# Late modulation vectors of a diffusion layer: from a matmul with ones to accumulating transfers and a row in DRAM

## The chip, the cores and the metric

The kernel runs on one core of a Trainium2 chip. The metric is the device time of one execution in microseconds, the median of several runs of the program. A profiled execution of the same program gives the trace; its time is given beside its span, which is the stretch from its first to its last instruction.

The engines are named as the profile names them: PE (TensorE matmul), PEld (its weight load), DVE (VectorE), ACT (ScalarE), POOL (GpSimd) and SP (SyncE, which only issues transfers here). POOL issues a few transfers as well.

## The reference

One layer with two token mixers and an MLP, on 256 latent tokens and 256 context tokens of 2048 channels. What concerns the change is how a conditioning vector becomes six modulation vectors of 2048 values each, and where four of them are used:

```python
mod = (jax.nn.silu(c) @ w_mod[l] + b_mod[l])[:, None, :]
sa, ca, ga, sm, cm, gm = jnp.split(mod, 6, axis=-1)
...
h = modulate(x, norm_attn_w[l], sa, ca)
p = h @ w_in[l]
...
x = x + ga * mix
x = x + gm * sq_relu_mlp(modulate(x, norm_mlp_w[l], sm, cm), w_ff1[l], w_ff2[l])
```

`modulate(x, w, shift, scale)` is `rmsnorm(x, w) * (1 + scale) + shift`. So `ga` and `gm` scale the two branches, `sm` shifts the MLP's input, and `cm` enters as `norm_mlp_w * (1 + cm)`. All inputs are float32.

## The kernel before

Tokens or weight columns are held in tiles of 128 partitions; almost all PE time goes into weight products. A weight chunk of 128 x 1024 float32 is loaded by SP into one of five `raw` buffers (`raw_chunk`), then split into a high part `whi` (an ACT cast to the matmul's float format, L243) and a low part `wlo` (a DVE subtraction, L244), each in three buffers. A product then takes three matmuls: high by high, low by high and high by low. The order of the chunks is the list `stream`; `wchunk` hands out the next one, loads two ahead, and calls `tick`, which counts down a list of delayed pieces of work (`later(n, fn)` puts one there, to be emitted n chunks later).

The instructions of one engine run in the order of the program on that engine. A scheduler chooses that order when the program is built, from the order of emission and its own estimate of times; `pin` keeps an instruction of an engine where it was emitted. Engines wait for each other through semaphores, and an instruction that waits holds everything behind it on its engine.

The stages in order of time are: the early modulation `sa`, `ca` together with the first q and k products (to about 122 us), values, keys, queries and attention, the pooling branch (`pin`, `za`, `pd`), the gates and up projections (`pg`, `pyy`), the output projection (`wo`), and the MLP (`f`, with first layer `ff1` and second layer `ff2` alternating in eight blocks).

The other four vectors are made late, in the shade of those stages, by `late_gen`. It works through `ga`, `cm`, `sm`, `gm`, each in two halves of 1024 columns. For a half it:

- clears an accumulator `macc` of 128 x 1024 on POOL (L618) and loads the bias into its partition 0 by a POOL transfer (L619);
- loads 16 weight chunks between those of `stream`, and adds each, times the 128 values of silu(c) that belong to it (one per partition, `sil`), into `macc` on DVE (`late_part`, L637). Afterwards the vector is the sum of `macc` over its partitions;
- splits `macc`, 512 columns at a time, into a high part `ah` (ACT, L270) and a low part `al` (DVE, L271), and multiplies both by a matrix of ones on PE into a PSUM bank (`late_sum`, L656 and L657). That sums over partitions and leaves the sum in all 128 at once;
- copies the bank to its place (ACT, L661), or, for `cm`, adds 1 and multiplies by the norm weight (DVE, L659). The norm weight `nmw` comes as four loads of 128 x 512, already repeated over partitions.

There is one `macc`, so a half can begin only when the half before it has been split. The results stand in `ga_bc`, `sb` (`cm` and `sm`) and `gm_bc`.

POOL does little: the last addition of the rotary embedding on q and k (`qraw`, L485), the clamp of squared attention outputs (`osq`, L740), the running sums of the pooling branch (`za`, L797 to L804), and the squares of the MLP (`rsq`, L1058). After such a square ACT casts it into the next block's operand `act` (L270), between its weight casts.

Of the kernel before, what the change touches and what calls it, by code (L numbers as in the profile page):

```python
# [48 lines left out]
def layer(ctx: ExitStack, tc, a, out):  # L49
    nc = tc.nc  # L50
    pool = ctx.enter_context(tc.tile_pool(name="sb", bufs=1))
    psum = ctx.enter_context(tc.tile_pool(name="ps", bufs=8, space=bass.MemoryType.PSUM))
    pe, gp = nc.tensor, nc.gpsimd
# [17 lines left out]
    def bank(name):  # L71
        return psum.tile([P, 512], F32, tag="ps", name=name)

    def work(name, shape=None, dt=F32):
        return pool.tile(shape or [P, 512], dt, tag="w2", name=name, bufs=9)
# [20 lines left out]
    def later(n, fn):  # L96

        waiting.append([n, fn])
# [170 lines left out]
    def split(hi, lo, src):  # L269
        act.copy(hi, src)  # L270
        vec.tensor_sub(lo, src, hi.bitcast(F32))  # L271
# [36 lines left out]
    ones = pool.tile([P, P], F32R, tag="ones", name="ones")  # L308
    vec.memset(ones.bitcast(F32), 1.0)
# [286 lines left out]
    parts = []  # L596

    def late_gen():
        for name in ("ga", "cm", "sm", "gm"):
# [11 lines left out]
            for half in range(2):  # L611
                yield
                for part in parts:
                    if part in waiting:
                        waiting.remove(part)
                        part[1]()
                acc = pool.tile([P, 1024], F32, tag="macc", name="macc", bufs=1)
                gp.memset(acc, 0.0)  # L618
                nc.gpsimd.dma_start(acc[0:1, :], a["b_" + name][half])  # L619
                norm_w = []  # L620
                for k in range(KT):
                    raw = raw_chunk(a["w_" + name][half, k])
                    if name == "cm" and k == 8:
                        for q in range(2):
                            norm_w.append(work("nmw"))
                            nc.gpsimd.dma_start(norm_w[q], a["nmw"][2 * half + q])
                    later(2 if credit_rate[0] < 1 else 1, partial(late_part, acc, raw, k))
                    parts.append(waiting[-1])
                    if k == KT - 1:
                        o = dst[:, half * 1024:half * 1024 + 1024]  # L630
                        later(2 if credit_rate[0] < 1 else 1, partial(late_split, acc, norm_w, o))
                        parts.append(waiting[-1])
                    yield

    def late_part(acc, raw, k):

        pin(vec.scalar_tensor_tensor(acc, raw, sil[:, 0, k:k + 1], acc, ALU.mult, ALU.add))  # L637

    def late_split(acc, norm_w, o):
        for q in range(2):  # L640
            part = partial(late_half, q, acc, norm_w, o)
            if q == 0:
                part()
            else:
                later(2, part)
                parts.append(waiting[-1])

    def late_half(q, acc, norm_w, o):
        ah, al = work("ah", dt=F32R), work("al", dt=F32R)
        split(ah, al, acc[:, q * 512:q * 512 + 512])  # L650
        later(3, partial(late_sum, ah, al, norm_w[q] if norm_w else None, o[:, q * 512:q * 512 + 512]))

    def late_sum(ah, al, wr, o):

        ps = bank("late")
        pin(pe.matmul(ps, ones, ah, start=True, stop=False))  # L656
        pe.matmul(ps, ones, al, start=False, stop=True)  # L657
        if wr is not None:
            vec.scalar_tensor_tensor(o, ps, 1.0, wr, ALU.add, ALU.mult)  # L659
        else:  # L660
            act.copy(o, ps)  # L661
# [452 lines left out]
def _layout(inp):  # L1114
# [17 lines left out]
    put("nmw", np.broadcast_to(f["norm_mlp_w"][0].reshape(4, 1, 512), (4, P, 512)))  # L1132
# [65 lines left out]
```

## Time and profile before

| What | Value |
|---|---|
| Time, median of 3 runs | 1466.71 us (1464.83 to 1470.06) |
| The profiled execution's own time | 1468.97 us |
| Its span | 1467.0 us |
| PE busy | 1442.9 us |
| DVE busy | 998.5 us |
| ACT busy | 684.7 us |
| POOL busy | 120.9 us |
| Moved by SP's queue | 345.51 MB |
| Moved by POOL's queue | 1.08 MB |

A group line of the profile reads: line, engine, operation, output <- inputs, shape, count, then busy time, mean length of one in ns, and the engine's idle time just before, with what ended it. A line of the timeline begins with the start and the length in us. Matmuls overlap in the pipeline, so the distance between their starts, not their length, is what one costs.

### The profile page before, as it was taken

What the parts mean: (1) busy time and instruction counts of PE and PEld (TensorE: products, weight loads), DVE (VectorE), ACT (ScalarE), POOL (GpSimd) and SP (SyncE); (2) the same over time, 40 slices, a digit from 0 to 9 for tenths busy, and PEclk for the clock granted to TensorE, in tenths of its full rate; (3) what the DMA queues carried; (4) which work ended last, traced back from release to release, by engine and by line L of the source; (5) the groups of instructions that cost most, each with busy time, mean ns of one, the idle gap of its engine ahead of it and who ended that gap; (6) DMA issues with size and microseconds to landing.
All of it is one profiled execution on the core that took longest, in us unless ns stands there. A gap on an engine that the chain in (4) does not pass through costs nothing.

```text
span 1467.0 us, 19801 instructions
## 1 busy us (share of the span) xinstructions
PE 1442.9 (98%) x7480; PEld 1186.6 (81%) x7480; DVE 998.5 (68%) x1239; ACT 684.7 (47%) x929; POOL 120.9 (8%) x120
## 2 busy tenths in 40 slices
PE   6999999999999999999999999999999999999998
PEld 4667887778878888888888888888888888888887
DVE  4568787768887786778676656666666655555675
ACT  5225346466554444445444554445344453544442
POOL 0001110101400000000001000001000000000260
PEclk9999999999999999999999999999999999999999
DMA  9996774435788878899646777777777655556554
GB/s 380 408 408 224 227 277 155 150 110 172 235 288 289 304 267 294 280 318 321 203 168 204 230 246 234 237 225 234 240 241 237 201 189 193 191 190 195 183 196 140
DMA packets 97439, 347.85 MB, mean 237 GB/s; under 512 B 11072, under 2 KB 11712, under 8 KB 97344
## 3 DMA queue, kind: packets, MB, share of 16 engines
q1 hardware_dynamic: 96768, 345.51, 69.8%
q8 instruction: 58, 0.95, 0.3%
q0 software_dynamic: 576, 1.08, 0.2%
q14 instruction: 37, 0.30, 0.1%
HBM read 344.45 MB, written 2.10 MB: 236 GB/s over the span
## 4 chain that ended last, share of the span: by engine, by line
PE 84%; DMA 9%; DVE 5%; ACT 1%; issue 1%; SPq 0%; POOL 0%; DVEq 0%; ACTq 0%; POOLq 0%
PE f L1047 14%; PE f L454 8%; PE f L455 8%; PE f L460 8%; PE f L1050 7%; DMA raw<-in_w_m_dram 6%; PE pg L454 3%; PE pg L455 3%; PE pg L460 3%; PE wo L454 2%; PE pyy L454 2%; PE wo L460 2%; PE pyy L460 2%; PE wo L455 2%; PE pyy L455 2%; PE v L455 2%
## 5 line engine op out<-in xcount | busy, mean ns | idle before, releaser
L244 DVE TENSOR_TENSOR wlo<-raw,whi 128x1024 fp32r<-128x1024 f32 (+1 forms) x430 | 534.7, 1245 | 345.3 <-ACT whi L243 321.8
L243 ACT CAST whi<-raw 128x1024 fp32r<-128x1024 f32 (+1 forms) x430 | 449.8, 1047 | 555.1 <-PE f L455 179.6
L1047 PE MATMUL f<-h,whi 128*128 128x512 f32 x896 | 224.3, 392 | 0.0
L455 PE MATMUL f<-whi,act 128*128 128x512 f32 x512 | 199.3, 389 | 0.0
L454 PE MATMUL f<-whi,act 128*128 128x512 f32 x512 | 199.3, 389 | 0.0
L1047 PEld LDWEIGHTS f<-h,whi 128*128 128x128 f32 x896 | 161.6, 189 | 29.2
L637 DVE SCALAR_TENSOR_TENSOR macc<-raw,sil,macc 128x1024 f32<-128x1024 f32 x128 | 164.9, 1289 | 3.1 <-issue 2.4
L460 PE MATMUL f<-wlo,act 128*128 128x512 f32 x512 | 136.8, 389 | 0.0
L1050 PEld LDWEIGHTS f<-h,wlo 128*128 128x128 f32 x896 | 122.2, 190 | 8.7
L1050 PE MATMUL f<-h,wlo 128*128 128x256 f32 x896 | 124.9, 282 | 0.0
L460 PEld LDWEIGHTS f<-wlo,act 128*128 128x128 f32 x512 | 96.1, 188 | 20.0
L455 PEld LDWEIGHTS f<-whi,act 128*128 128x128 f32 x512 | 96.2, 188 | 19.8
L454 PEld LDWEIGHTS f<-whi,act 128*128 128x128 f32 x512 | 96.2, 188 | 19.8
L454 PE MATMUL pg<-whi,hL 128*128 128x512 f32 x256 | 101.5, 396 | 0.0
L455 PE MATMUL pg<-whi,hL 128*128 128x512 f32 x256 | 100.3, 392 | 0.0
L1058 POOL TENSOR_TENSOR rsq<-relu 128x512 f32<-128x512 f32 x28 | 29.2, 1042 | 527.5 <-ACT relu L1057 497.0
L460 PE MATMUL pg<-wlo,hL 128*128 128x512 f32 x256 | 68.6, 390 | 0.0
L454 PEld LDWEIGHTS pg<-whi,hL 128*128 128x128 f32 x256 | 48.6, 190 | 10.5 <-ACT whi L243 0.2
L455 PEld LDWEIGHTS pg<-whi,hL 128*128 128x128 f32 x256 | 48.5, 189 | 10.4 <-issue 0.2
L460 PEld LDWEIGHTS pg<-wlo,hL 128*128 128x128 f32 x256 | 48.0, 188 | 10.4 <-DVE wlo L244 0.4
L618 POOL MEMSET macc<- 128x1024 f32 x8 | 7.6, 955 | 488.6 <-DVE al L271 375.4
L1072 DVE TENSOR_TENSOR acc<-f,acc 128x512 f32<-128x512 f32 x48 | 30.9, 686 | 19.6 <-PE f L460 19.6
(275 smaller groups left out, 2104.9 us busy)
## 6 DMA issues: line engine op xcount, KB each, us to landing
raw<-in_w_ff_dram SPq DMA_DIRECT2D x240, 512.0 KB, 4.1
raw<-in_w_m_dram SPq DMA_DIRECT2D x64, 512.0 KB, 10.2
raw<-in_w_ga_dram SPq DMA_DIRECT2D x32, 512.0 KB, 4.5
raw<-in_w_cm_dram SPq DMA_DIRECT2D x32, 512.0 KB, 4.6
raw<-in_w_gb_in_dram SPq DMA_DIRECT2D x32, 512.0 KB, 4.7
raw<-in_w_ga_in_dram SPq DMA_DIRECT2D x32, 512.0 KB, 5.1
raw<-in_w_sm_dram SPq DMA_DIRECT2D x32, 512.0 KB, 4.9
raw<-in_w_o_dram SPq DMA_DIRECT2D x32, 512.0 KB, 4.4
```

The source lines that it names most:

```text
L243: act.copy(hi, raw)
L244: vec.tensor_sub(lo, raw, hi.bitcast(F32))
L454: pe.matmul(banks[t], tok(h, k, 0, tt), wt, start=k == 0, stop=False)
L455: pe.matmul(banks[t], tok(h, k, 1, tt), wt, start=False, stop=False)
L460: pe.matmul(banks[t], tok(h, k, 0, tt), wt, start=False, stop=k == 2 * nk - 1)
L618: gp.memset(acc, 0.0)
L637: pin(vec.scalar_tensor_tensor(acc, raw, sil[:, 0, k:k + 1], acc, ALU.mult, ALU.add))
L1047: pe.matmul(ps, hi[:, kk * P:kk * P + P], both(h2, k), start=k == 0, stop=False)
L1050: pe.matmul(ps[:, T:2 * T], lo[:, kk * P:kk * P + P], act_slice(h2, k, 0), start=False, stop=k == KT - 1)
L1058: gp.tensor_mul(sq, r, r)
L1072: vec.tensor_add(acc[:, t, gs], bs[t], acc[:, t, gs])
```

## The change

The products of `late_part` now go straight into the half of `ga_bc`, `sb` or `gm_bc` where the result belongs; `macc` and its splitting, the matrix of ones and the matmuls are gone. The sum over partitions is made by seven transfers that POOL issues: the upper 64 partitions are added onto the lower 64, then 32 onto 32, and so on to one (`late_fold`). For `cm`, POOL adds 1 to that one row and multiplies it by the norm weight, which is now loaded as a row. The row is then written to DRAM (`row`) and read back into all 128 partitions. Each of these steps is emitted one chunk after the last, and each waits for the one before to have landed.

```diff
+    rows = ctx.enter_context(tc.tile_pool(name="rows", bufs=2, space=bass.MemoryType.DRAM))
...
-    ones = pool.tile([P, P], F32R, tag="ones", name="ones")
-    vec.memset(ones.bitcast(F32), 1.0)
...
-                for part in parts:
-                    if part in waiting:
-                        waiting.remove(part)
-                        part[1]()
-                acc = pool.tile([P, 1024], F32, tag="macc", name="macc", bufs=1)
-                gp.memset(acc, 0.0)
-                nc.gpsimd.dma_start(acc[0:1, :], a["b_" + name][half])
-                norm_w = []
+                o = dst[:, half * 1024:half * 1024 + 1024]
+                gp.memset(o, 0.0)
+                nc.gpsimd.dma_start(o[0:1, :], a["b_" + name][half])
+                norm_w = None
                 for k in range(KT):
                     raw = raw_chunk(a["w_" + name][half, k])
                     if name == "cm" and k == 8:
-                        for q in range(2):
-                            norm_w.append(work("nmw"))
-                            nc.gpsimd.dma_start(norm_w[q], a["nmw"][2 * half + q])
-                    later(2 if credit_rate[0] < 1 else 1, partial(late_part, acc, raw, k))
+                        norm_w = pool.tile([P, 1024], F32, tag="macc", name="nmw", bufs=1)[0:1, :]
+                        nc.gpsimd.dma_start(norm_w, a["nmw"][half])
+                    later(2 if credit_rate[0] < 1 else 1, partial(late_part, o, raw, k))
                     if k == KT - 1:
-                        later(2 if credit_rate[0] < 1 else 1, partial(late_split, acc, norm_w, o))
+                        later(2 if credit_rate[0] < 1 else 1, partial(late_fold, o, norm_w, P // 2))
...
-    def late_sum(ah, al, wr, o):
-        ps = bank("late")
-        pin(pe.matmul(ps, ones, ah, start=True, stop=False))
-        pe.matmul(ps, ones, al, start=False, stop=True)
-        if wr is not None:
-            vec.scalar_tensor_tensor(o, ps, 1.0, wr, ALU.add, ALU.mult)
-        else:
-            act.copy(o, ps)
+    def late_fold(o, norm_w, n):
+        if n > 0:
+            nc.gpsimd.dma_start(o[0:n, :], o[n:2 * n, :], accum_op=ALU.add)
+            later(1, partial(late_fold, o, norm_w, n // 2))
+            return
+        if norm_w is not None:
+            gp.tensor_scalar(o[0:1, :], o[0:1, :], 1.0, None, ALU.add)
+            gp.tensor_mul(o[0:1, :], o[0:1, :], norm_w)
+        row = rows.tile([1, 1024], F32, tag="row", name="row")
+        nc.gpsimd.dma_start(row, o[0:1, :])
+        later(1, lambda: nc.gpsimd.dma_start(o, row.broadcast_to([P, 1024])))
```

The new code lies 21 lines higher in most of the program, so L1058 is L1037 there, and L740 is L719. On PE the order of everything else is the same as before. This is PE in the gate stage, where the first half of `cm` is summed; `pg0` and `pg1` are the two banks of a gate product. Before:

```order
L460 MATMUL pg0_3991<-wlo_4037,hL1_731 128x512
L460 MATMUL pg1_3992<-wlo_4037,hL1_731 128x512
L656 MATMUL late_4108<-ah_4041,ones_70 128x512
L657 MATMUL late_4108<-al_4042,ones_70 128x512
L454 MATMUL pg0_3991<-whi_4059,hL1_731 128x512
L455 MATMUL pg0_3991<-whi_4059,hL1_731 128x512
L454 MATMUL pg1_3992<-whi_4059,hL1_731 128x512
L455 MATMUL pg1_3992<-whi_4059,hL1_731 128x512
```

The same place in the changed program:

```order
L459 MATMUL pg0_3974<-wlo_4020,hL1_731 128x512
L459 MATMUL pg1_3975<-wlo_4020,hL1_731 128x512
L453 MATMUL pg0_3974<-whi_4039,hL1_731 128x512
L454 MATMUL pg0_3974<-whi_4039,hL1_731 128x512
L453 MATMUL pg1_3975<-whi_4039,hL1_731 128x512
L454 MATMUL pg1_3975<-whi_4039,hL1_731 128x512
```

The pair of `late` between two weight chunks is gone, and the next chunk follows directly.

POOL's queue around the end of `ga`'s second half, where the pooling branch begins (`za` are its running sums, `osq` the clamped squares of attention outputs). Before:

```order
L740 TENSOR_SCALAR osq_2577<-osq_2577 128x512
L618 MEMSET macc_2926 128x1024
L619 DMA macc_2926<-in_b_cm_dram 1x16x64
L797 MEMSET za_2990 128x8
L798 MEMSET za_2990 128x8
L797 MEMSET za_2995 128x8
L798 MEMSET za_2995 128x8
L740 TENSOR_SCALAR osq_2917<-osq_2917 128x512
L804 TENSOR_TENSOR za_2990<-za_2990 128x271
```

In the changed program, where the folds of 64 and 32 partitions stand just ahead of the first row:

```order
L632 DMA ga_bc_1338<-ga_bc_1338 16x1024
L632 DMA ga_bc_1338<-ga_bc_1338 8x1024
L632 DMA ga_bc_1338<-ga_bc_1338 4x1024
L612 MEMSET sb_2805 128x1024 x2
L613 DMA sb_2805<-in_b_cm_dram 1x16x64
L776 MEMSET za_2974 128x8
L777 MEMSET za_2974 128x8
L776 MEMSET za_2979 128x8
L777 MEMSET za_2979 128x8
L632 DMA ga_bc_1338<-ga_bc_1338 2x1024
L719 TENSOR_SCALAR osq_2904<-osq_2904 128x512
L613 DMA sb_2805<-in_b_cm_dram 1x16x64
```

Five folds now stand ahead of the clearing of `sb` and of the bias load of `cm`, and a sixth ahead of the second `osq`.

POOL's queue in the MLP, around the end of `gm`'s second half. Before, only the squares stand there:

```order
L1058 TENSOR_TENSOR rsq2_9503<-relu_9504 128x512
L1058 TENSOR_TENSOR rsq2_9609<-relu_9610 128x512
L1058 TENSOR_TENSOR rsq2_10042<-relu_10043 128x512
L1058 TENSOR_TENSOR rsq2_10145<-relu_10146 128x512
L1058 TENSOR_TENSOR rsq2_10248<-relu_10249 128x512
```

In the changed program:

```order
L1037 TENSOR_TENSOR rsq2_9559<-relu_9560 128x512
L632 DMA gm_bc_6629<-gm_bc_6629 64x1024
L632 DMA gm_bc_6629<-gm_bc_6629 32x1024
L632 DMA gm_bc_6629<-gm_bc_6629 16x1024
L632 DMA gm_bc_6629<-gm_bc_6629 8x1024
L632 DMA gm_bc_6629<-gm_bc_6629 4x1024
L632 DMA gm_bc_6629<-gm_bc_6629 2x1024
L632 DMA gm_bc_6629<-gm_bc_6629 1x16x64
L639 DMA row_9916<-gm_bc_6629 16x1x64
L1037 TENSOR_TENSOR rsq2_9986<-relu_9987 128x512
L640 DMA gm_bc_6629<-row_9916 128x1024
L1037 TENSOR_TENSOR rsq2_10089<-relu_10090 128x512
```

Seven folds and the write of the row come between two squares, the second of which ACT waits for; the read back comes between the next two.

More of the change, by code (lines that the diff above doesn't have):

```diff
@@ L595, in layer @@
     ga_bc = s8("ga_bc", [P, D])
-    parts = []
     def late_gen():
@@ L623, in late_gen @@
                     if name == "cm" and k == 8:
-                        for q in range(2):
-                            norm_w.append(work("nmw"))
-                            nc.gpsimd.dma_start(norm_w[q], a["nmw"][2 * half + q])
-                    later(2 if credit_rate[0] < 1 else 1, partial(late_part, acc, raw, k))
-                    parts.append(waiting[-1])
+                        norm_w = pool.tile([P, 1024], F32, tag="macc", name="nmw", bufs=1)[0:1, :]
+                        nc.gpsimd.dma_start(norm_w, a["nmw"][half])
@@ L629, in late_gen @@
+                    later(2 if credit_rate[0] < 1 else 1, partial(late_part, o, raw, k))
                     if k == KT - 1:
-                        o = dst[:, half * 1024:half * 1024 + 1024]
-                        later(2 if credit_rate[0] < 1 else 1, partial(late_split, acc, norm_w, o))
-                        parts.append(waiting[-1])
+                        later(2 if credit_rate[0] < 1 else 1, partial(late_fold, o, norm_w, P // 2))
                     yield
-    def late_part(acc, raw, k):
-        pin(vec.scalar_tensor_tensor(acc, raw, sil[:, 0, k:k + 1], acc, ALU.mult, ALU.add))
@@ L639, in late_split @@
[L639 to L643, printed above, removed]
-            else:
[L645 to L651, printed above, removed]
@@ L653, in late_sum, with late_part @@
-    def late_sum(ah, al, wr, o):
-        ps = bank("late")
-        pin(pe.matmul(ps, ones, ah, start=True, stop=False))
-        pe.matmul(ps, ones, al, start=False, stop=True)
-        if wr is not None:
-            vec.scalar_tensor_tensor(o, ps, 1.0, wr, ALU.add, ALU.mult)
-        else:
-            act.copy(o, ps)
+    def late_part(o, raw, k):
+        pin(vec.scalar_tensor_tensor(o, raw, sil[:, 0, k:k + 1], o, ALU.mult, ALU.add))
+    def late_fold(o, norm_w, n):
[9 more added lines that the diff above has]
+        later(1, lambda: nc.gpsimd.dma_start(o, row.broadcast_to([P, 1024])))
@@ L1131, in _layout @@
         put("b_" + n, bm[chunk[n]].reshape(2, 1, 1024))
-    put("nmw", np.broadcast_to(f["norm_mlp_w"][0].reshape(4, 1, 512), (4, P, 512)))
+    put("nmw", f["norm_mlp_w"][0].reshape(2, 1, 1024))
     wi = f["w_in"][0]
```

## The prediction

> **What bounds the kernel now.** I read the page first: busy time by engine and the chain that ended last.
>
> ```profile
> span 1467.0 us, 19801 instructions
> PE 1442.9 (98%) x7480; PEld 1186.6 (81%) x7480; DVE 998.5 (68%) x1239; ACT 684.7 (47%) x929; POOL 120.9 (8%) x120
> PE 84%; DMA 9%; DVE 5%; ACT 1%; issue 1%; SPq 0%; POOL 0%; DVEq 0%; ACTq 0%; POOLq 0%
> ```
>
> TensorE is busy 98% of the span and holds 84% of the chain; POOL holds 0% of it. A stage view shows where that is complete.
>
> ```profile
> 398.00:440.00 42.00, 39.04 (x170) 31.40 (x170) 34.79 (x40) 22.15 (x27) 1.19 (x2) 0.97 0.86 291
> 440.00:760.00 320.00, 319.99 (x1426) 263.88 (x1425) 236.67 (x244) 145.57 (x173) 5.72 (x9) 1.00 0.81 274
> 760.00:1160.00 400.00, 400.00 (x2024) 339.95 (x2024) 262.13 (x272) 191.94 (x237) 23.73 (x22) 1.00 0.71 230
> ```
>
> The columns are the length, then PE, PEld, DVE, ACT and POOL busy, the granted clock, the DMA share and GB/s. From 440 to 1160 us PE has no idle time: a matmul that goes away there is time that goes away, provided nothing new makes PE wait. At 398 to 440 us PE is idle for 3 us and the transfers are at their densest, 0.86.
>
> **What goes: 32 matmuls.** Next I looked at the tile `late`, its times in windows, and PE's timeline around one pair.
>
> ```profile
> L656 PE MATMUL late<-ah,ones 128*128 128x512 f32 x16 | 6.8, 426 | 2.1 <-ACT ah L270 2.1
> 440.00:760.00 320.00, 4.66 (x14) 2.55 (x14) 2.24 (x4) 2.36 (x4) 1.00 0.81 274
> 760.00:1160.00 400.00, 2.54 (x8) 1.50 (x8) 0.00 (x0) 2.35 (x4) 1.00 0.71 230
> 206.30 0.62 PE L460 MATMUL k<-wlo,hC 128*128 128x512 f32 x2
> 206.75 0.40 PE L656 MATMUL late<-ah,ones 128*128 128x512 f32 x1
> 206.99 0.40 PE L657 MATMUL late<-al,ones 128*128 128x512 f32 x1
> 207.22 0.39 PE L454 MATMUL k<-whi,hL 128*128 128x512 f32 x1
> 207.45 0.39 PE L455 MATMUL k<-whi,hL 128*128 128x512 f32 x1
> ```
>
> The mean of 426 ns is the pipelined length, not the price. The price is the distance of starts: from 206.75 to 207.22 a pair takes 0.47 us. The two windows (here of the tile alone) hold 14 + 8 = 22 of the 32 matmuls, so 11 pairs lie where PE never idles: 11 x 0.47 = **5.2 us**, the firmest term. Of the five others, four belong to the gate vector `ga` (200 to 330 us) and one, the first pair of `cm`, stands at 436 us:
>
> ```profile
> 433.67 1.05 ACT L243 CAST whi<-raw 128x1024 fp32r<-128x1024 f32 x1 [2.29 <-DMA raw<-in_w_ga_in_dram]
> 434.95 1.04 ACT L243 CAST whi<-raw 128x1024 fp32r<-128x1024 f32 x1 [0.23 <-DMA raw<-in_w_ga_in_dram]
> 435.90 1.14 ACT L270 CAST ah<-macc 128x512 fp32r<-128x512 f32 x2
> 433.38 1.07 PE L460 MATMUL pg<-wlo,hL 128*128 128x512 f32 x4
> 436.57 0.50 PE L656 MATMUL late<-ah,ones 128*128 128x512 f32 x1 [2.12 <-ACT ah L270]
> 437.91 0.80 PE L657 MATMUL late<-al,ones 128*128 128x512 f32 x1 [0.84 <-DVE al L271]
> 438.50 0.63 PE L454 MATMUL pg<-whi,hL 128*128 128x512 f32 x1
> 438.93 0.63 PE L455 MATMUL pg<-whi,hL 128*128 128x512 f32 x1
> 441.02 0.39 PE L454 MATMUL pg<-whi,hL 128*128 128x512 f32 x1
> ```
>
> Four matmuls from 433.38 at 0.227 us would let the next one start at 434.29; it starts at 438.50, 4.2 us later, because PE, in order, stands at `late` until ACT and DVE have made its two operands. Behind it six matmuls start 0.42 us apart until 441.02 (2.52 us for what takes 1.36): another 1.2 us after the idle time. Together 5.4 us. Without the pair PE next waits for the cast that ends at 433.67 + 1.05 = 434.72, so at most 4.9 us come back. The lower bound is the plain 0.47 us, if the transfers of that stage then hold PE anyway. The following cast (434.95) was ready before PE, a chunk of 12 matmuls or 2.7 us later, would ask for it, so I take **4.5 us**, near the upper end. The four `ga` pairs are worth 4 x 0.47 = 1.9 us at most, but all come before the cast at 433.67 that waited for a weight transfer, so the gain may only lengthen that wait: 0 to 1.9, I take **0.3**. The casts `ah`, the differences `al` and the copies out of PSUM leave ACT and DVE, which are idle 53% and 32% of the time; I count nothing for that (at best one DVE weight difference less in front of a chunk, about 1.2 us, at worst as much lost by a changed order). Sum of the gains: 5.2 + 4.5 + 0.3 = **10.0 us**.
>
> **What comes: 72 transfers on POOL's queue, each waiting for the last.** A half now takes seven accumulating folds, one write of the row and one broadcast, in POOL's program order with POOL's other work. No accumulating transfer is in the trace; the nearest rows are POOL's own small loads:
>
> ```profile
> L619 POOL DMA_DIRECT2D macc<-in_b_gm_dram x2: 487/514/540, 683.0 to 955.4; - x2
> DMA to landing us min/median/max: 1.8/3.7/5.2
> nmw<-in_nmw_dram POOLq DMA_DIRECT2D x4, 256.0 KB, 4.7
> ```
>
> An issue costs POOL about 0.5 us; a 4 KB load lands 1.8 to 5.2 us after its issue, a 256 KB load after 4.7. A fold moves 256, 128, ... 4 KB. So a step, issue to next issue, is bounded by 1.9 and 5.3 us; I take **3.8** (the median and a tenth for the semaphore), since most folds are as small as those loads. POOL elsewhere has long gaps (8% busy); two places decide. First the second half of `gm`:
>
> ```profile
> 1138.38 1.28 DVE L637 SCALAR_TENSOR_TENSOR macc<-raw,sil,macc 128x1024 f32<-128x1024 f32 x1
> 1167.90 1.04 POOL L1058 TENSOR_TENSOR rsq<-relu 128x512 f32<-128x512 f32 x1 [54.53 <-ACT relu L1057]
> 1168.98 0.62 ACT L270 CAST act<-rsq 128x512 fp32r<-128x512 f32 x1 [0.21 <-POOL rsq L1058]
> 1170.15 1.05 ACT L243 CAST whi<-raw 128x1024 fp32r<-128x1024 f32 x1 [0.55 <-PE f L1047]
> 1168.06 2.00 PE L1047 MATMUL f<-h,whi 128*128 128x512 f32 x8
> 1170.86 2.00 PE L1047 MATMUL f<-h,whi 128*128 128x512 f32 x8
> 1176.44 2.00 PE L1047 MATMUL f<-h,whi 128*128 128x512 f32 x8
> ```
>
> The last product lands in the sum at 1139.66. Seven folds and the issue of the row stand ahead of the square of 1167.90 in POOL's order; two `late` pairs fall away in between, so the square is due at 1166.96. That is 27.3 us, 3.9 us a step for no delay. If the square is late, ACT stands at its cast of it, and the weight cast of 1170.15 queues behind. PE takes a chunk every 2.80 us and `whi` has three buffers, so that cast is for the chunk of 1176.44 and has 1176.44 - 1171.20 = 5.2 us to spare. PE loses from (27.3 + 5.2) / 7 = **4.6 us a step** on, 7 us for each us beyond. Second, the second half of `ga`:
>
> ```profile
> 305.63 1.27 DVE L637 SCALAR_TENSOR_TENSOR macc<-raw,sil,macc 128x1024 f32<-128x1024 f32 x1
> 329.63 1.28 DVE L637 SCALAR_TENSOR_TENSOR macc<-raw,sil,macc 128x1024 f32<-128x1024 f32 x1
> 326.53 1.49 POOL L740 TENSOR_SCALAR osq<-osq 128x512 f32<-128x512 f32 x1 [0.37 <-ACT osq L739]
> 337.57 1.02 PE L744 MATMUL osum<-osq,mean 128*128 128x512 f32 x2
> ```
>
> Four landings, the fifth issue (0.5), two clears of `sb` (1.9, by 0.96 each) and the bias load's landing (1.8 at best) now stand between the end of `ga`'s products, 306.90, and the first product of `cm` in DVE's order, 329.63: 311.1 + 4 steps, again 4.6 us a step. The clamp `osq` stands behind a fifth landing, and its product on PE at 337.57 allows 5.6. With 3.8 neither place costs anything: I take 0, with bounds of 0 and, at 5.3, 7 x 0.7 + 4 x 0.7 = 7.7 us. The POOL products on the row, the writes and the broadcasts end chains whose readers come 100 us and more later; they cost nothing but traffic.
>
> The row that prices an issue beside a busy DVE is the 487 to 540 ns above. The Trainium skill, "SBUF — State Buffer", section "SBUF: two separate sides", speaks against the change: it says that POOL cannot write a transfer's descriptors while DVE runs certain copies, and gives about 620 ns alone and 3100 ns beside one. By its figures an estimate of a step is 3.8 + 2.5 = 6.3 us, and the sum would be a loss; this trace's issues do not show such a stretch.
>
> The sum is made against the profiled execution's 1468.97 us (span 1467.0): 1459.0. That execution lies 2.3 us above the median of the three runs, 1466.71, and nothing in its rows looks peculiar to it, so the forecast for the median is 1466.7 - 10 = **1457 us**.
>
> **Rivals.**
> - *Only the firm term.* The transfers at 398 to 440 us hold PE as soon as `late` is gone. For it: the DMA share of 0.86 and the cast that waited 2.29 us for a load. Against it: the next weight cast waited just 0.23 us for its load and was in time. Gain 5.2 us: 1461.5.
> - *The chain of folds takes `late`'s place as the wait, and the kernel is slower.* An accumulating transfer reads its destination as well, so a step could take 6 us. Then the square of `gm` costs 7 x 1.4 = 9.8 us and `cm`'s first product 4 x 1.4 = 5.6: 1456.7 + 15.4 = 1472. It decides from 4.6 us a step and turns the sign near 5.5. Against it: no POOL load here took over 5.2.
> - *DVE holds up the issues.* If an issue had to outlast two DVE instructions (1.23 us for a weight difference and 1.28 for a product), a step is 3.8 + 2.5 = 6.3 us: 11 x 1.7 = 18.7 us lost, 1475. Against it: the issues of 0.5 us, with DVE busy two thirds of the time. [...]
> - *The folds' traffic delays weights.* A half moves 0.5 MB of folds and 0.5 MB of broadcast; four halves fall where the DMA share is 0.81 and add about 4 MB, less 1 MB of `nmw`, to 320 us at 274 GB/s: 0.84. If the largest fold and the broadcast push one weight chunk back so that PE waits 1.5 us in each, a third of the 4.7 us row: 6 us lost, 1463. For it: little slack at 434. Against it: 0.84 is below the 0.86 at which PE idled only at `late`.
>
> **How the numbers follow.** Forecast as worked out (1453 to 1461): 0.62. Firm term only: 0.12, still faster. Traffic: 0.12, within 0.3% (4.4 us, about what a measurement of this kernel tells from no change). Long steps: 0.10, of which 0.02 ends within 0.3%. DVE: 0.04. So faster 0.74, same 0.14, slower 0.12. The range goes from 1452 (both upper bounds, 5.2 + 4.9 + 1.9 + 1.2, and the runs' own scatter) to 1468 and leaves out the two slow rivals.
>
> **What would show it.** Right: no `late` on PE, no gap and full clock at 434 to 441 us, steps under 4.6 us between POOL's folds, the square after `gm`'s last fold starting with ACT's relu. Wrong: POOL waiting for a landing while ACT's cast of the square or DVE's first `cm` product waits for POOL, with PE idle behind them at about 1175 or 330 us; or weight casts in 440 to 760 us that wait longer for their loads.

## The result, and the profile after

| Kernel | Median | Lowest to highest | Runs |
|---|---|---|---|
| before | 1467.49 us | 1464.63 to 1471.82 | 20 |
| changed | 1470.53 us | 1466.92 to 1476.48 | 20 |

The changed kernel takes 1.0025 times the time of the kernel before (95% interval 1.0014 to 1.0036), so it is 3.0 us slower by the medians. The forecast was 1457 us, the range ended at 1468. The profiled execution of the changed kernel took 1473.67 us, 3.1 us more than its median, and that of the kernel before 1468.97 us, 1.5 us more than its own. So the two traces lie 4.7 us apart where the medians lie 3.0 apart, and times read from single traces need not add up to differences of medians.

The page of the changed kernel begins:

```profile
span 1471.9 us, 19792 instructions
PE 1437.8 (98%) x7448; PEld 1180.0 (80%) x7448; DVE 993.6 (68%) x1218; ACT 669.8 (46%) x901; POOL 182.5 (12%) x194
```

PE has 5.1 us less to do, as the 32 matmuls would make one expect, in a span that is 4.9 us longer. So PE now waits some 10 us more. The same three stages as in the prediction, in the view by windows (length, busy time of PE, PEld, DVE, ACT, POOL, granted clock, DMA share, GB/s):

```profile
398.00:440.00 42.00, 42.00 (x190) 34.62 (x189) 35.38 (x39) 21.54 (x26) 0.92 (x1) 1.00 0.84 283
440.00:760.00 320.00, 312.53 (x1380) 255.73 (x1379) 231.93 (x228) 136.63 (x158) 41.03 (x44) 0.99 0.86 288
760.00:1160.00 400.00, 400.00 (x2020) 339.40 (x2020) 263.10 (x274) 189.32 (x232) 31.30 (x32) 1.00 0.72 233
```

The 3 us of idle PE at 398 to 440 us are gone. In their place PE is idle for 7.5 us between 440 and 760 us, where it was never idle before, and runs 1380 matmuls there instead of 1426. The timeline of PE in the changed kernel, cut to the first matmul after the five gaps that matter (the bracket holds the idle time before it and what ended it):

```profile
216.78 0.44 PE L491 MATMUL qkT<-prm,qraw 128*128 128x128 f32 x2 [2.19 <-POOL qraw L484]
...
489.99 0.50 PE L453 MATMUL pyy<-whi,yb 128*128 128x512 f32 x1 [1.32 <-ACT whi L244]
...
569.12 0.50 PE L459 MATMUL pg<-wlo,hL 128*128 128x512 f32 x1 [1.62 <-DVE wlo L245]
...
577.96 0.80 PE L453 MATMUL pg<-whi,hL 128*128 128x512 f32 x1 [2.21 <-ACT whi L244]
...
1181.26 0.50 PE L1026 MATMUL f<-h,whi 128*128 128x512 f32 x1 [1.29 <-ACT whi L244]
```

Where time comes from and goes to is read best by following the same matmul through two traces. This table has, for a few matmuls, its start in the trace of before, and how much later (+) or earlier (-) it starts in the changed kernel and in two of the experiments below (the first 100 us, the same in all, differ by up to 2 us from one execution to the next, so only the steps down a column count):

```
start before, us   changed   e4_bare   e7_ga_gm
        207.2        +0.7      +1.4      -0.4
        330.2        +1.7      +0.1      +0.6
        431.4        +2.9      +1.3      +1.2
        440.6        -2.4      -3.9      -4.1
        495.9        +0.1      -4.6      -4.3
        576.4        +6.2      -5.5      -4.8
        689.2        +3.8      -7.8      -6.7
       1151.4        +3.4      -9.7      -8.6
       1178.1        +4.9      -9.7      -5.4
       1460.0        +4.9      -9.7      -4.6
```

The changed kernel gains 5.3 us at 436 us and then loses 8.6 us up to 576 us. After that it gains again as the matmuls fall away, and loses 1.5 us at 1178 us (and 1.4 us near 753 us, which was not followed up).

### The profile page after: what moved, and what is told of

It reads as the page before. It is cut to its first block, busy times and chain, and to the rows that moved or that the text cites. A ratio compares the mean times of both kernels' runs of the same rounds, so it can differ in the third digit from the quotient of the medians.

```text
span 1471.9 us, 19792 instructions
## 1 busy us (share of the span) xinstructions
PE 1437.8 (98%) x7448; PEld 1180.0 (80%) x7448; DVE 993.6 (68%) x1218; ACT 669.8 (46%) x901; POOL 182.5 (12%) x194
## 3 DMA queue, kind: packets, MB, share of 16 engines
HBM read 347.61 MB, written 2.13 MB: 238 GB/s over the span
## 5 line engine op out<-in xcount | busy, mean ns | idle before, releaser
L627 DVE SCALAR_TENSOR_TENSOR sb<-raw,sil,sb 128x1024 f32<-128x1024 f32 x64 | 88.1, 1377 | 1.6 <-DMA sb<-in_b_cm_dram 1.6
L1037 POOL TENSOR_TENSOR rsq<-relu 128x512 f32<-128x512 f32 x28 | 29.2, 1042 | 429.4 <-ACT relu L1036 419.2
L632 POOL DMA_DIRECT2D sb<-sb x28 | 22.2, 793 | 261.4 <-DVE sb L627 150.2
```

The source lines that it names most:

```text
L627: pin(vec.scalar_tensor_tensor(o, raw, sil[:, 0, k:k + 1], o, ALU.mult, ALU.add))
L632: nc.gpsimd.dma_start(o[0:n, :], o[n:2 * n, :], accum_op=ALU.add)
L1037: gp.tensor_mul(sq, r, r)
```

## Experiments

All runs are one table. "PE idle" is 320 us less PE's busy time in the window from 440 to 760 us of the profiled execution; "POOL's queue" is the share of the 16 DMA engines' time that the transfers issued by POOL took from 440 to 600 us. Each kernel was timed against the kernel before on the same chip; in the kernel before the two figures are 0 us and 0.9%. From e1 to e7, and in e9, e13, e14, e17 and e18, parts of the summing are left out or changed, so the late vectors are not the right sums there. A difference of two medians below is uncertain by 2 to 3 us, by these intervals.

| Run | Median | Before | Ratio, 95% interval | PE idle | POOL's queue |
|---|---|---|---|---|---|
| changed | 1470.5 | 1467.5 | 1.0025 (1.0014 to 1.0036) | 7.5 | 6.7% |
| e1_no_spread | 1464.0 | 1468.6 | 0.9979 (0.9967 to 0.9990) | 3.1 | 3.5% |
| e2_no_norm | 1467.8 | 1468.6 | 1.0001 (0.9990 to 1.0012) | 2.8 | 5.7% |
| e3_no_folds | 1458.3 | 1468.6 | 0.9938 (0.9923 to 0.9953) | 0 | 3.1% |
| e4_bare | 1458.2 | 1468.6 | 0.9931 (0.9917 to 0.9946) | 0 | 0 |
| e5_folds_only | 1464.5 | 1468.4 | 0.9969 (0.9957 to 0.9981) | 2.3 | 3.9% |
| e6_plain | 1468.1 | 1468.4 | 0.9997 (0.9987 to 1.0008) | 4.7 | 4.0% |
| e7_ga_gm | 1462.9 | 1468.4 | 0.9952 (0.9935 to 0.9968) | 0.2 | 2.2% |
| e8_before_later | 1466.3 | 1468.4 | 0.9987 (0.9975 to 0.9998) | 0.2 | 1.3% |
| e9_spread3 | 1465.7 | 1468.1 | 0.9982 (0.9970 to 0.9994) | 3.5 | 6.0% |
| e10_squares_dve | 1472.1 | 1468.1 | 1.0025 (1.0010 to 1.0040) | 4.8 | 4.7% |
| e11_free_dve | 1477.8 | 1468.1 | 1.0067 (1.0052 to 1.0082) | 17.7 | 4.3% |
| e12_hybrid | 1464.2 | 1468.1 | 0.9978 (0.9969 to 0.9986) | 1.5 | 1.0% |
| e13_fold64 | 1467.3 | 1467.2 | 1.0000 (0.9992 to 1.0009) | 6.2 | 3.1% |
| e14_fold63 | 1463.3 | 1467.2 | 0.9974 (0.9961 to 0.9988) | 2.3 | 4.1% |
| e15_best | 1460.4 | 1467.2 | 0.9953 (0.9941 to 0.9965) | 0.1 | 1.1% |
| e16_before_adds | 1464.0 | 1467.2 | 0.9977 (0.9966 to 0.9987) | 0.5 | 0.1% |
| e17_only64 | 1458.6 | 1467.8 | 0.9939 (0.9925 to 0.9952) | 0 | 1.8% |
| e18_only63 | 1457.5 | 1467.8 | 0.9935 (0.9922 to 0.9949) | 0.4 | 1.9% |

### The three added parts, one at a time and all together

Three theories stood after this reading: S, the spread's 512 KB delay the weights; R, POOL's arithmetic on the row slows DVE; F, the folds.

**e1_no_spread.**

```diff
-        row = rows.tile([1, 1024], F32, tag="row", name="row")
-        nc.gpsimd.dma_start(row, o[0:1, :])
-        later(1, lambda: nc.gpsimd.dma_start(o, row.broadcast_to([P, 1024])))
+        later(1, lambda: None)
```

> The changed kernel without the write of the summed row and without its spreading back over the partitions: each late vector stays as the folds leave it. All other steps stay at their places. Theory S (the 512 KB spread is what delays the weights: while it runs, from 479.3 to 487.4 and from 568.6 to 576.6 us, loads land 7.4 to 7.8 us after their issue and not 5.4): PE's gaps at 490.0 (1.3 us) and 578.0 (2.2 us) go, and the 1.4 us lost at the lower clock behind the second, so about 4.9 us less than the changed kernel, 1465.6. Theory R (POOL's arithmetic on one row slows DVE, and the slots of the loads come free late): the gap at 569.1 (1.6 us) stays and most of that at 490.0 too; 1469 to 1470. Theory F (the folds, their waits and their traffic): no change by more than 1 us.

1464.0 us, 6.5 less. The size is what S gave and more, but the gaps did not all go: PE is still idle for 3.1 us from 440 to 760 us.

**e2_no_norm.**

```diff
-        if norm_w is not None:
-            gp.tensor_scalar(o[0:1, :], o[0:1, :], 1.0, None, ALU.add)
-            gp.tensor_mul(o[0:1, :], o[0:1, :], norm_w)
```

> The changed kernel without POOL's two operations on the summed row of the third vector (the addition of one and the norm weight): the spread row is the plain sum. Theory R: DVE's products beside them take 1.28 us again and not 3.43, 5 us of DVE come back, and the gaps at 490.0 (1.3 us), 569.1 (1.6 us) and 578.0 (2.2 us, and 1.4 us of lower clock behind it) go: 6.5 us less, 1464. Theory S: the spreads only come 6 us earlier, and their two gaps stay, 1468 to 1470. Theory F: no change by more than 1 us.

1467.8 us, 2.7 less, at the edge between R (1464) and S (1468 to 1470). What R meant is plain in the changed kernel's timelines of POOL and of DVE around one row:

```profile
470.39 3.52 POOL L636 TENSOR_SCALAR sb<-sb 1x1024 f32<-1x1024 f32 x1 [3.78 <-DMA sb<-sb]
...
474.00 2.72 POOL L637 TENSOR_TENSOR sb<-sb,nmw 1x1024 f32<-1x1024 f32 x1
...
474.38 3.43 DVE L627 SCALAR_TENSOR_TENSOR sb<-raw,sil,sb 128x1024 f32<-128x1024 f32 x1
```

The product of DVE, 1.28 us elsewhere, takes 3.43 and ends 1.09 us after POOL's multiplication does (474.38 + 3.43 = 477.81; 474.00 + 2.72 = 476.72). Its slot of `raw` comes free late, and the next load of the list is issued at 477.83.

**e3_no_folds** and **e4_bare.** The first drops the transfer below, the second all three parts.

```diff
         if n > 0:
-            nc.gpsimd.dma_start(o[0:n, :], o[n:2 * n, :], accum_op=ALU.add)
             later(1, partial(late_fold, o, norm_w, n // 2))
```

> The changed kernel without the 7 accumulating transfers of each half: row 0 is multiplied, written and spread as it is, right after the last product. Theory F in its small form (only POOL's waits): the gaps at 216.8 (2.2 us, POOL's part of q queued behind two folds) and at 1181.3 (1.3 us, the square behind seven) go, with 549.0 (0.7 us): 4.2 us less, 1466. In its large form (the folds' traffic makes the whole loss between 446 and 580 us): 4 us and up to 8 more, 1459 to 1462. Theories R and S: only the small form's share, with stalls of 4 to 6 us left near 440 and 520 us, where row arithmetic and spread now begin right behind the last product.

> The changed kernel with only the direct accumulation left: no folds, no row arithmetic, no spread, so that the late vectors are not summed. It shows the gain before any cost. By my forecast's sum (5.2 us of matmuls after 440 us, 4.5 us of the stall at 436 us, 0.3 us before): 10 us below the kernel before, 1457.5. If the cost is not in these three parts but in the direct accumulation itself (another order of DVE, other slots), it stays at 1463 or above.

Both take 1458.3 and 1458.2 us, and PE has no idle time between 440 and 760 us in either. So the gain of the change is 10.4 us (forecast 10.0). Row arithmetic and spread without folds cost nothing measurable, although the spread is the same 0.5 MB a half. The whole cost of 12.3 us (1470.5 - 1458.2) appears only once the folds are there, and it is not a sum: leaving out the spread alone takes 6.5 us off it, leaving out the row arithmetic alone 2.7, leaving out the folds alone 12.2. These runs come from different chips, on which the kernel before takes 1467.2 to 1468.6 us. Counted against the kernel before on its own chip, e4 is 10.4 us faster and the changed kernel 3.0 us slower, a cost of 13.4 us.

**e5_folds_only** has e2's and e1's edits together.

> The changed kernel with the direct accumulation and the folds, without row arithmetic and without spread. Without anything the run before this one measured 1458.2 us, with row arithmetic and spread but no folds 1458.3, with folds and row arithmetic 1464.0. Theory F1 (the folds cost by themselves, through POOL's waits and their traffic, and the spread adds only where it meets them): 1462 to 1464. Theory I (folds alone are free too, only the three together are too much): 1458 to 1460.

1464.5: folds alone cost 6.3 us. F1 holds; theory I falls.

### Where the folds cost

**e7_ga_gm.** `cm` and `sm`, the two vectors of 440 to 760 us, start at the row at once:

```diff
-partial(late_fold, o, norm_w, P // 2)
+partial(late_fold, o, norm_w, P // 2 if name in ("ga", "gm") else 0)
```

> The changed kernel with folds for the first and the last vector only; the two vectors of the stretch from 440 to 760 us are multiplied and spread without folds. Theory D (the cost lies where the DMA queues are already at 0.85 to 0.95): 1462 (1458.3 without any folds, and 2.2 us at 217 and 1.3 us at 1181 us for POOL's queue), no gap left between 440 and 760 us. Theory P (POOL's queue makes most of the cost, wherever the folds are): 1466 or above.

1462.9, and 0.2 us of idle PE from 440 to 760 us, as theory D said. So the 12.3 us divide by place: 7.6 for the folds of `cm` and `sm` (1470.5 - 1462.9), 4.6 for those of `ga` and `gm` (1462.9 - 1458.3). Counted against the kernel before of each, the shares are 8.5 and 4.8. The steps in the table by matmuls show where the second part is. From 207 to 441 us e7 gains 3.7 us and e4 5.3, so most of e7's gap of 2.2 us at 216 us (POOL's addition of q, behind the folds) stays lost. From 441 to 1151 us it gains 4.5 us and e4 5.8. From 1151 us to the end it falls back by 4.0 us, where e4 loses nothing. PE in e7:

```profile
1170.16 0.50 PE L1026 MATMUL f<-h,whi 128*128 128x512 f32 x1 [2.17 <-ACT whi L244]
```

and POOL in the changed kernel at the same place:

```profile
1170.60 0.77 POOL L632 DMA_DIRECT2D gm_bc<-gm_bc  x1 [3.01 <-DMA gm_bc<-gm_bc]
1175.01 0.79 POOL L632 DMA_DIRECT2D gm_bc<-gm_bc  x1 [3.64 <-DMA gm_bc<-gm_bc]
1178.01 0.53 POOL L639 DMA_DIRECT2D row<-gm_bc  x1 [2.21 <-DMA gm_bc<-gm_bc]
1178.55 1.06 POOL L1037 TENSOR_TENSOR rsq<-relu 128x512 f32<-128x512 f32 x1
```

with ACT beside it:

```profile
1170.56 0.63 ACT L1036 ACTIVATE relu<-f1s 128x512 f32<-128x512 f32 x1 [1.35 <-DVE f1s L1033]
...
1179.64 0.62 ACT L271 CAST act<-rsq 128x512 fp32r<-128x512 f32 x1 [7.51 <-POOL rsq L1037]
```

The operand of the square is ready at 1171.2; POOL gets to it at 1178.55, behind seven folds, and ACT stands for 7.51 us at the cast that needs it.

**e10_squares_dve** takes the square out of POOL's queue.

```diff
-            gp.tensor_mul(sq, r, r)
+            vec.tensor_mul(sq, r, r)
```

> The changed kernel with the 28 squares of the last stage on DVE and not on POOL; PE's, ACT's and SP's orders stay. If the loss at 1181 us (1.3 us of gap, 1.4 us in all; 2.2 and 2.7 us in the run with folds for the first and last vector only) is the square queued behind seven folds on POOL, it goes: 1.4 to 2.7 us less than the changed kernel, 1468 to 1469, with no gap between 1140 and 1200 us. If the folds hold up something else there (the weights' transfers), the gap stays and the time is 1470 to 1471.

In its trace PE has no idle time from 760 to 1200 us. That alone does not show that the gap was the square behind the folds, for e1, e5, e6 and e14 keep the square there and have no idle time either. What tells the runs apart is the time from the end of the last product of `gm` to the square. It is 31.3 us in e1, 31.8 in e5, 32.7 in e6 and 31.6 in e14. It is 34.6 in the changed kernel, 34.3 in e2 and 35.5 in e7, and only in these three PE has a gap there (1.3, 1.0 and 2.2 us). The prediction's limit for this time, 27.3 + 5.2 = 32.5 us, lies between the two groups, but for e6, which is just beyond it. So the gap is the square's wait, once the chain of folds is too long. The median of e10 does not show the gain, 1472.1 us with runs from 1464.5 to 1475.6. Its runs are 11.1 us apart, as those of the changed kernel are (9.6 us; e4 4.2 us), so on the time this run is inconclusive.

**e11_free_dve** moves the additions of q and k and the norm weight to DVE too.

```diff
-            gp.tensor_add(raw, raw, sq)
+            vec.tensor_add(raw, raw, sq)
...
-            gp.tensor_scalar(o[0:1, :], o[0:1, :], 1.0, None, ALU.add)
-            gp.tensor_mul(o[0:1, :], o[0:1, :], norm_w)
+            vec.scalar_tensor_tensor(o[0:1, :], o[0:1, :], 1.0, norm_w, ALU.add, ALU.mult)
```

> The same with, in addition, the additions of q and k on DVE and the third vector's norm weight as one operation of DVE on the row in place of POOL's two. What the runs so far put on POOL then goes: 2.7 us for the row arithmetic, 1.4 to 2.7 for the square, up to 2.2 for q. If these add up: 1463 to 1465, and what is left above 1458 is the folds' own part between 440 and 760 us. If the folds' traffic fills each hole, 1466 to 1469. DVE has some 32% of the span idle, but the attention part is reordered, which may cost a microsecond or two.

A miss, 1477.8 us. DVE works in order too, and now it stands at the row until the last fold has landed; in its timeline:

```profile
462.11 1.21 DVE L636 SCALAR_TENSOR_TENSOR sb<-sb,nmw 1x1024 f32<-1x1024 f32 x1 [5.96 <-DMA sb<-sb]
```

Two such waits leave PE idle for 7.7 us each, at 464 and 555 us. The operation itself is 1.21 us against POOL's 6.2. Up to 441 us this run was 10.4 us ahead of the kernel before, which led to e15 and e16.

### What the folds take between 440 and 760 us

**e6_plain** keeps every transfer and wait, without accumulation.

```diff
-nc.gpsimd.dma_start(o[0:n, :], o[n:2 * n, :], accum_op=ALU.add)
+nc.gpsimd.dma_start(o[0:n, :], o[n:2 * n, :])
```

> The changed kernel with the same 7 transfers of each half, same sizes, same order and same waits, but copying instead of accumulating, so that the late vectors are not sums. Theory A (the accumulation makes the transfers slow: a step of 4.75 us at the last half, and 25 us of all DMA engines' time for 4.2 MB): a step falls to 3 us or less and the time to 1460 to 1464. Theory T (any chain of small transfers through POOL's queue does this, by bytes and waits): steps and time stay, 1469 to 1471.

1468.1, nearer to T, with a part for A. The view of the line in e6 and in the changed kernel (issue on POOL in ns, and landing in us):

```profile
L632 POOL DMA_DIRECT2D gm_bc<-gm_bc x14: 488/510/587, 953.5 to 1169.7; - x14
...
DMA to landing us min/median/max: 2.0/4.2/8.6
```

```profile
L632 POOL DMA_DIRECT2D gm_bc<-gm_bc x14: 759/780/882, 957.0 to 1175.0; - x14
...
DMA to landing us min/median/max: 2.3/4.7/8.3
```

Accumulating adds 0.27 us to an issue and 0.5 us to a landing; a plain chain would have been almost as long.

**e9_spread3** has no folds, and three spreads in place of one.

```diff
-        later(1, lambda: nc.gpsimd.dma_start(o, row.broadcast_to([P, 1024])))
+        later(1, lambda: [nc.gpsimd.dma_start(o, row.broadcast_to([P, 1024])) for _ in range(3)])
```

> The kernel without folds (1458.3 us), and each row spread three times in place of once. The two added spreads take about as much of the DMA engines as the folds did: 1.7% of the span, 25 us, for the folds of 8 halves, 3.1 us a half; 0.9%, 13 us, for 8 spreads, so 3.3 us a half for two more. Theory C (the cost between 440 and 760 us is DMA time, whatever moves): 1462 to 1466, with gaps in that stretch. Theory L (the folds cost by another way than their DMA time: where they stand, or how long they last): 1458 to 1460, no gaps.

1465.7, as theory C said: transfers of another kind cost the like once there are as many. The view of the DMA queues from 440 to 600 us (packets, MB, share of 16 engines) shows what gives way. In e4, with no added transfer, and then in the changed kernel:

```profile
q1 hardware_dynamic: 13327, 48.52, 89.0%
```

```profile
q1 hardware_dynamic: 12340, 44.94, 81.0%
q0 software_dynamic: 949, 2.06, 6.7%
```

`q1` carries the weights. Its share and POOL's add up to 89.0% in e4, 89.0 in e3, 89.4 in e5, 89.5 in e9 and 87.7 in the changed kernel: a sum that hardly moves, in which 6.7% for POOL's queue goes with 3.6 MB less weights, seven chunks. Of the other runs with folds or spreads in this stretch, e11, whose DVE stands at the row, has 79.8%; the rest lie between 86.0% (e13) and 90.3% (e2). That the sum has a ceiling is a reading that fits these numbers; no run raises it further and shows it. In e4 the 89.0% are enough for a PE that never waits. For the kernels that accumulate directly, the table's last two columns then read as a threshold. Up to 3.1% (e4, e17, e18, e7, e3) PE has at most 0.4 us of idle time; from 3.5% on it has 2.3 to 7.5 us. Two runs do not fit: e11, whose idle time is DVE's wait for the folds, and e13, with 6.2 us at 3.1%. So the threshold is a reading too.

**e13_fold64, e14_fold63**, and the same without row arithmetic and spread, **e17_only64, e18_only63**: the first fold of each half alone, or the six others alone.

```diff
-            nc.gpsimd.dma_start(o[0:n, :], o[n:2 * n, :], accum_op=ALU.add)
+            _ = n == P // 2 and nc.gpsimd.dma_start(o[0:n, :], o[n:2 * n, :], accum_op=ALU.add)
```

This is e13's edit. e14 has `n < P // 2`, and e17 and e18 are the same two edits of e5.

> The changed kernel with only the first fold of each half (64 rows, 256 KB of the 508 KB); the sums stay incomplete. Without folds 1458.3, with all seven 1470.5. Theory B (bytes): half of the cost, 1463 to 1466. Theory N (the number of transfers and their waits): 1458 to 1461.

> The changed kernel without the first fold of each half, with the six others (32 rows to 1, 252 KB). Theory B: half of the cost, 1463 to 1466, like the run with the first alone. Theory N: nearly all of it, 1467 to 1470, since six of the seven steps and 26 of the 33 us of the chain stay.

> Direct accumulation and the first fold of each half alone (64 rows); no other fold, no row arithmetic, no spread. Theory B (bytes): half of the 6.3 us that all seven cost without row arithmetic and spread, 1461 to 1462. Theory N (number): 1458 to 1459. If one transfer of 7 us right behind the last product is the worst by its size: 1463 to 1465.

> Direct accumulation and the six smaller folds of each half (32 rows to 1) alone; no row arithmetic, no spread. Theory B: 1461 to 1462, like the first alone. Theory N: 1463 to 1465. If only a transfer as large as the first costs: 1458 to 1460.

Either half of the folds alone costs nothing that these runs can tell (1458.6 and 1457.5, e4 1458.2), all seven cost 6.3. Theory N falls by e18. Theory B (1461 to 1462 for each) lies just above the intervals, which end at 1460.8 us for e17 and 1460.3 for e18. The reading that fits is that the stretch has room for a half, not for the whole. The traces, one execution each, are less clear-cut: from 441 us on e4 gains 5.8 us on the kernel before, e17 4.6, e18 4.2 and e5 1.6, so each half may cost a little. e14, with its 4.1%, lies above that room and costs 5.0 us. e13 costs 9.0 us at 3.1%; there the row arithmetic follows right behind the last product. Its DVE:

```profile
445.59 3.23 DVE L245 TENSOR_TENSOR wlo<-raw,whi 128x1024 fp32r<-128x1024 f32 x1
```

and its PE:

```profile
448.88 0.50 PE L459 MATMUL pyy<-wlo,oT 128*128 128x512 f32 x1 [0.97 <-DVE wlo L245]
```

The weight difference, 1.23 us elsewhere, took 3.23 beside POOL's multiplication, and PE waited for it. A second wait of 1.2 us for DVE followed at 465 us. In the second half of `cm` a DVE operation of 0.68 us took 2.57 beside POOL's multiplication, and PE waited 0.93 us for DVE at 534 us. That shows one part of e13's loss. But in e3 such hold-ups cost nothing, and why the first fold with row and spread costs more than six folds with them was not settled.

### Kernels that beat both

**e8_before_later** is the kernel before, with `cm`'s summing matmuls three steps later.

```diff
-        later(3, partial(late_sum, ah, al, ...
+        later(6 if norm_w else 3, partial(late_sum, ah, al, ...
```

> The kernel before, with the matmuls that sum the third vector set three steps later in the order; nothing else is changed. If the gaps of 2.1 and 0.8 us at 436 us, and the lower clock behind them, come from PE reaching the first of these matmuls before ACT has cut the accumulated row, they go: 4.5 us less than the kernel before, 1464. If another wait ends at the same time (the weights that land at 434 to 437 us), the gap moves to the weights' matmuls and the time stays at 1467 to 1469.

1466.3. The gaps at 436 us are gone from its trace, and a matmul that started at 440.6 us is 5.2 us early; at the end of the trace 4.0 us of that are left. By the medians 2.1 us stay (0.3 to 3.7 by the interval), less than the 4.5 expected.

**e12_hybrid** adds folds for `gm` alone, with the squares on DVE; **e15_best** adds the additions of q and k on DVE; **e16_before_adds** is the kernel before with those additions moved and nothing else.

```diff
-                acc = pool.tile([P, 1024], F32, tag="macc", name="macc", bufs=1)
+                o = dst[:, half * 1024:half * 1024 + 1024]
+                acc = o if name == "gm" else pool.tile([P, 1024], F32, tag="macc", name="macc", bufs=1)
...
-                        later(2 if credit_rate[0] < 1 else 1, partial(late_split, acc, norm_w, o))
+                        fold = partial(late_fold, o, P // 2) if name == "gm" else partial(late_split, acc, norm_w, o)
+                        later(2 if credit_rate[0] < 1 else 1, fold)
...
-            gp.tensor_mul(sq, r, r)
+            vec.tensor_mul(sq, r, r)
```

(with e8's edit, and `late_fold` as in the changed kernel without the norm weight). In e15 and e16:

```diff
-            gp.tensor_add(raw, raw, sq)
+            vec.tensor_add(raw, raw, sq)
```

> The kernel before with three edits: the third vector's summing matmuls three steps later (2.1 us less by itself), folds and spread for the last vector only, and the squares on DVE so that nothing waits on POOL behind the folds. The last vector's 4 pairs of matmuls are worth 1.9 us; together 1464.5, if the folds of this stretch (DMA share 0.70 to 0.72) are free. If they are not: 1466 to 1468.

> The hybrid (1464.2: third vector's matmuls three steps later, folds for the last vector alone, squares on DVE) with the additions of q and k on DVE too. If the gain that e11 showed between 210 and 440 us (5 us more than the run with the direct accumulation alone) comes from that move: 1459 to 1460. If it came from the absence of folds' neighbours there: 1463 to 1465.

> The kernel before with only the additions of q and k on DVE and not on POOL. By the gap at 273.9 us (2.5 us, PE waits for ACT's e) that was gone in e11, and the lead that grew there: 1463 to 1465 against 1467.5. If that gain needs the direct accumulation: 1466 to 1469.

1464.2, 1460.4 and 1464.0. In e12's trace PE gains 1.9 us on the kernel before between 900 and 1151 us, as in e4, where four pairs of `gm` fall away, and loses nothing up to the end. So by the trace folds pay there, where the DMA share is 0.74 and nothing waits behind them on POOL. By the medians e12 is 3.9 us below its kernel before and e8 2.1, which the intervals do not tell apart, and the squares on DVE without folds were not tried. e15 is 0.9953 of the time before (0.9941 to 0.9965); of its 6.8 us about 3 are the additions' move, which has nothing to do with the change.

## Why the prediction was wrong

Step by step, by its own terms:

- **Eleven pairs, 5.2 us: right.** In e4, from 441 us to the end, the lead grows by 5.8 us (-3.9 to -9.7).
- **The stall at 436 us, 4.5 us: right in the traces.** In the changed kernel PE goes through 398 to 440 us without a gap at full clock, and its lead grows by 5.3 us there, pair included, a little above the prediction's bound of 4.9. By the medians e8, which takes away this wait alone and keeps the pair, gains 2.1 us (0.3 to 3.7), so the usual run of the kernel before may lose less there than its profiled one.
- **Four `ga` pairs, 0.3 us, and ACT's and DVE's relief, 0:** nothing speaks against it. The sum, 10.0 us, was measured as 10.4 (e4). That it comes so close is partly luck, since e8 leaves the second term in doubt.
- **A step of a fold, 3.8 us: too short.** At `gm`'s second half seven steps take 33.2 us (1144.27 to 1177.47), 4.75 us each, and 4.4 at `ga`'s second half; these lie within the bounds. Between 440 and 760 us the mean step of a half is 4.8 to 5.8 us, at the longest beyond the bound of 5.3. The small folds took little more than the small loads had suggested, the largest much more: at `gm`'s second half the first two steps take 7.3 and 5.6 us, the other five 3.0 to 5.0. The turning point of 4.6 us a step was right: 7 x 0.15 = 1.0 us was to be lost at 1175 us, the gap is 1.3 us there, and nothing was lost at 330 us. In e7 the same place cost 4.0 us.
- **"They cost nothing but traffic": the step that failed.** The term of 0 us for the added transfers and the row was wrong by 12.3 us, or 13.4 against the kernel before of each run, which with the gain of 10.4 makes the 3.0 us of the result. Some 4.6 of it (4.8) come from `ga` and `gm`: the square's place behind `gm`'s folds was seen and priced at 0, by too short a step, and the addition of q behind `ga`'s first half (2.2 us of idle PE) was not seen. The other 7.6 (8.5) come from the folds of `cm` and `sm`, between 440 and 760 us, where two things were overlooked. The traffic was weighed by its bytes and as a mean, 0.84 against a stall's 0.86 in an earlier stage. But an accumulating fold takes half as much again of the DMA engines as a plain transfer of its size, and where the weights are densest, from 440 to 600 us, the queues' shares add up to 0.85 in the kernel before, to 0.89 in e4 without any added transfer, and to 0.90 at most in any run. By the table there is room for some 3%, and the change asks for 6.7; e9, with two more spreads in place of the folds, shows that traffic alone can cost as much (7.4 us), while e13 shows that 3% is no firm limit. And POOL's two operations on one row were counted as free because their reader comes late, while they held up DVE, by 2.15 us at one product and 0.78 and 2.13 at two others. Without folds beside them, in e3, hold-ups of 0.8 and 1.5 us cost nothing.
- **The rival "traffic delays weights", 1463 us with 0.12, named the right place** and the signs to look for (weight casts that wait longer: ACT waits 45.0 us in all for the loads `raw<-in_w_ga_in_dram` between 440 and 760 us, 35.0 before). It priced 1.5 us for the largest fold and the spread of each half and left out what they do together. One such meeting in the changed kernel, on POOL and on ACT:

```profile
568.55 0.57 POOL L640 DMA_DIRECT2D sb<-row  x1 [2.02 <-DMA row<-sb]
```

```profile
576.87 1.04 ACT L244 CAST whi<-raw 128x1024 fp32r<-128x1024 f32 x1 [7.64 <-DMA raw<-in_w_ga_in_dram]
```

  The spread begins with the lead already spent by the folds and the row, the next weights land 7.7 us after their issue, ACT waits 7.64 us, and PE 2.2 us, with the clock below full after it (0.98 on average from 520 to 600 us).
- **The rivals "long steps" (6 us) and "DVE holds up the issues" (6.3 us) did not happen.** Long steps did not come at the two places that it priced (4.75 and 4.4 us a step); `cm`'s second half, which it did not price, came near with 5.8. No issue of a fold took over 0.92 us. That the time, 1470.5 us, ended near 1472 is no point for long steps: it came by another way.

What stays open: how the 7.6 us divide among folds, row and spread, because the three are not additive; whether the room for transfers has a sharp edge; e13's excess over e14; and why the changed kernel and e10 scatter by 10 us from run to run.

## What to carry to other kernels

Work that is taken off a busy engine and given to transfers is free only as long as the transfers of that very stretch have room. The nearest sign of it here was the queues' summed share where the weights are densest, not a mean over the stage. Add the parts one by one and together: each half of the folds alone cost nothing that could be measured, all seven cost 6 us. On an in-order queue, look behind a chain of waits, on POOL for what stands after it, and on DVE before the work is moved there.

## What the runs showed of the hardware

- Two operations of POOL on a single row of 1024 took 2.6 to 3.5 us each, against 1.04 us for its product and 1.51 for its operation with a scalar on 128x512, which has half the columns. Per column, one partition is not cheaper than 128.
- Beside such a multiplication with both inputs in SBUF, DVE's two-input operation waited: 3.43 and 3.41 us instead of 1.28, ending 1.09 us after POOL's in each case (1.08 or 1.09 us also in e1, e3, e7, e13 and e14). The Trainium skill, "SBUF — State Buffer", section "SBUF: two separate sides", has a lock between these two engines that is held for a whole instruction; those two rows agree. Beside the addition of one, a DVE product took 2.06 us and ended 0.65 us before POOL's did, and other DVE operations beside it kept their usual length, which does not look like a lock for the whole instruction.
- An accumulating transfer within SBUF took half as much again of the DMA engines as a plain one of the same size: POOL's queue had 2.6% of the span in the changed kernel and 2.0% in e6, of which 0.9% are the spreads (e3), so 1.7 against 1.1%.
